# The order of the instructions made by a timeline simulation, in a one-block hybrid kernel

## The chip, the core and the metric

The kernel runs on one core of a Trainium2 chip. The core has five engines, each with an instruction queue of its own that is worked off in order: PE (TensorE, matmuls; its weight loads are listed apart, as PEld), DVE (VectorE), ACT (ScalarE), POOL (GpSimd) and SP (SyncE, which here only issues DMAs). An instruction waits at the head of its queue until the instructions of other engines that it depends on are done, and everything behind it in that queue waits with it. PE writes its results into PSUM, from where DVE and ACT take them to SBUF. The metric is the time of the program on the device in microseconds.

## The reference

One block on 512 tokens of width 1024, with 16 meta tokens put in front: a norm, an input projection, a gated linear recurrence, a retention (linear attention with decay) of 4 heads, a gated mix of the two, and a feed-forward part with a short convolution. All is float32.

```python
xn = rms_norm(h, norm_mix_g[l])
z = xn @ w_in[l]
u_rnn, u_gate, q, k, v, g_ret, ga, gb = jnp.split(z, IN_SPLITS, axis=-1)
xr = causal_dwconv(u_rnn, rnn_conv_w[l], rnn_conv_b[l])
hr = rg_lru(xr, rg_a_w[l], rg_a_b[l], rg_x_w[l], rg_x_b[l], lru_lambda[l])
o_a = hr * jax.nn.gelu(u_gate)
q = rotary(q.reshape(bsz, t, RET_HEADS, RET_DK), pos)
k = rotary(k.reshape(bsz, t, RET_HEADS, RET_DK), pos) * (RET_DK ** -0.5)
o = retention(q, k, v.reshape(bsz, t, RET_HEADS, RET_DV))
o_b = head_rms(o).reshape(bsz, t, RET_HEADS * RET_DV) * jax.nn.silu(g_ret)
mixed = (jax.nn.sigmoid(ga) * (o_a @ w_branch_rnn[l]) + jax.nn.sigmoid(gb) * (o_b @ w_branch_ret[l]))
h = h + mixed @ w_out[l]
xn = rms_norm(h, norm_ffn_g[l])
up = causal_dwconv(xn @ w_up[l], ffn_conv_w[l], ffn_conv_b[l])
gate, val = jnp.split(up, 2, axis=-1)
h = h + (jax.nn.gelu(gate) * val) @ w_down[l]
out = rms_norm(h, norm_final_g)[:, N_META:]
```

## The kernel before

**Numbers.** A float32 operand is split into two float16 parts, a high and a low one (`split`, L91 to L93): ACT writes the high part (L92), DVE the rest (L93). A product is then three passes: high by high, high by low, low by high. Weights come from memory as float32 tiles named `raw`, are split into tiles named `wt`, and stay only as long as they are used; so a stream of weight splits runs on ACT and DVE beside all other work. For some weights sums of blocks are made first (L255 to L257), for a scheme in which 7 block products do the work of 8; `fast_products` (L836), `up_products` (L1314) and the down projection (L1412) use it, the first with tiles `pa`, `pe`, `pb` in PSUM, from which ACT (`kept`, `last`, L849 and L1325) and DVE (`g`, L866, L870, L877) take the sums.

**Stages** (times of the profiled execution, in us): first norm and convolution of the recurrence (0 to 110, L515 to L665), its gates (to 150, L691), rotary products for q and k (145 to 230, `rotary` L720, products in `project` L395, DVE rows L736 to L738), scores and values (230 to 290), values, retention and gated units by head (to 430; values L907, the short product for the meta tokens L899, the sum of squares over a head L944, retention L929), mix units (430 to 650, branch products `pm` L395), output projection (650 to 700, L1180), up projection with its convolution (700 to 955; product L395 or L408, the first tap of the convolution on ACT L1295, the two others on DVE L1297), down projection (955 to 1054, L1417), and a last block of four plain products (L1429) with the final norm and the output (L1513 to L1532).

**Buffers.** PSUM tiles come from pools with few slots: `acc` has 4 slots in the rotary stage (L663), 2 in the gated units beside 4 single banks (L1014), 3 from the output projection on (L1170). A product that takes a slot waits until the last reader of the tile that had it is done. Weight tiles come from a pool of 10 (L60).

**What sets the order.** The kernel is written with a tile framework: the program text names operations in one order, and the framework then orders each engine's queue itself, by priorities and an account of what each instruction takes and when it could start. Two things limit it. From L477 to L713 (`tc.manual_schedule`) the order of PE, DVE and ACT is that of the program text; that part ends near 150 us. And single calls are held with `tc.issue_after` (the loads, L102) or put forward with `tc.high_priority` (L1187, L1251, L1324, L1328). The rows between are free to move. For the up projection two generators give rows in between: `x2_sums` (L1206) makes the sums of normalised activations (`x2t`, L1214 and L1216) and splits them (`x2f`, L93), and `x2_whole` (L1198, row L1204) the sums of high and low part they start from. The last four plain products are written in the order spare, P1, P6, P7 (L1514; spare is the second half of the tile P3).

## Time and profile before

| | |
|---|---|
| median of 3 runs | 1072.78 us (1072.77 to 1072.82) |
| the profiled execution | 1072.88 us, its span 1071.2 us |
| PE busy | 1051.1 us, 8995 matmuls |
| DVE busy | 863.1 us, 1297 instructions |
| ACT busy | 584.1 us, 903 instructions |
| mean granted PE clock | 0.999 of full speed |
| last matmul ends | 1064.6 us |

Busy times are sums over the span from the first to the last instruction. A group of rows is one line, engine and tile; a row of the timeline has start, length, engine, line, the tiles written and read, shapes, a count, and in brackets the idle time before it with what ended it. Rows that follow each other on DVE overlap by some 0.08 us, so the step from one start to the next is a little shorter than the length shown. A wait is counted at the engine that was idle.

### The profile page before, as it was taken

To read this page: it belongs to the slowest core of one execution; us is meant where nothing else is said; L and a number is where in the kernel's file an instruction comes from. 1 tells how busy PE (TensorE), PEld (TensorE's weight loads), DVE (VectorE), ACT (ScalarE), POOL (GpSimd) and SP (SyncE) were. 2 spreads that over 40 slices of the span, in tenths; PEclk is the share of its full clock that TensorE was granted. 3 is DMA by queue.
4 is the path that set the end of the run, shared out by engine and by line. 5 is a ranking of instruction groups with operands and counts; after the bars stand their busy time and mean duration, and the time that the engine had idled before them with its cause. 6 is when DMAs were issued, how large, how long until landed. Compare 5 with 4: busy or idle time off the path is not lost.

```text
span 1071.2 us, 20996 instructions
## 1 busy us (share of the span) xinstructions
PE 1051.1 (98%) x8995; PEld 851.3 (79%) x8995; DVE 863.1 (81%) x1297; ACT 584.1 (55%) x903; POOL 6.9 (1%) x20
## 2 busy tenths in 40 slices
PE   9999999999999999999999999999999999999997
PEld 6888888865684858888888885588888888888884
DVE  6884799998786969877797785599888887988875
ACT  8558954434564747566454453364555465454442
POOL 2000000000000000000000000000000000000000
PEclk9999999999999999999999999999999999999999
DMA  8341243431212222423333355032331423214322
GB/s 254 105 133 41 80 138 119 159 120 40 80 41 69 90 64 65 128 90 119 103 104 119 119 199 176 33 124 74 126 119 62 137 80 119 80 59 131 107 80 79
DMA packets 108990, 111.49 MB, mean 104 GB/s; under 512 B 5611, under 2 KB 100561, under 8 KB 108897
## 3 DMA queue, kind: packets, MB, share of 16 engines
q1 hardware_dynamic: 108448, 109.74, 31.8%
q8 instruction: 70, 1.15, 0.5%
q10 hardware_dynamic: 160, 0.27, 0.1%
q0 software_dynamic: 288, 0.14, 0.1%
q14 instruction: 24, 0.19, 0.1%
HBM read 108.04 MB, written 2.10 MB: 103 GB/s over the span
## 4 chain that ended last, share of the span: by engine, by line
PE 73%; DVE 16%; ACT 9%; issue 2%; ACTq 0%; DVEq 0%
PE ps L395 28%; PE P L1417 9%; PE pa L844 9%; PE pm L395 4%; PE ps L907 4%; PE ps L1180 4%; DVE wt L93 4%; PE pe L844 4%; PE ps L408 2%; PE pb L844 2%; ACT wt L92 2%; PE pa L1319 2%; PE ps L929 1%; DVE rnn L642 1%; DVE raw L255 1%
## 5 line engine op out<-in xcount | busy, mean ns | idle before, releaser
L395 PEld LDWEIGHTS <-wt 128*128 128x128 f16 x3840 | 373.2, 97 | 58.2 <-DVE t L736 1.4
L93 DVE SCALAR_TENSOR_TENSOR wt<-raw,wt 128x1024 f16<-128x1024 f32 (+2 forms) x278 | 303.8, 1105 | 69.1 <-ACT wt L92 68.0
L92 ACT ACTIVATE wt<-raw 128x1024 f16<-128x1024 f32 (+2 forms) x278 | 262.9, 961 | 152.6 <-PE P L1417 25.3
L844 PEld LDWEIGHTS <-wt 128*128 128x128 f16 x2016 | 195.1, 97 | 34.7 <-issue 7.4
L395 PE MATMUL ps<-x2h,wt 128*128 128x258 f16 x1184 | 182.0, 273 | 0.0
L395 PE MATMUL ps<-xh,wt 128*128 128x257 f16 (+2 forms) x1056 | 163.8, 275 | 1.1 <-DVE t L736 1.1
L395 PE MATMUL ps<-x2l,wt 128*128 128x258 f16 x592 | 113.3, 272 | 0.0
L395 PE MATMUL ps<-xl,wt 128*128 128x257 f16 (+2 forms) x528 | 102.2, 275 | 0.0
L1417 PE MATMUL P<-wt,act 128*128 128x256 f16 x792 | 88.3, 273 | 0.0
L1417 PEld LDWEIGHTS <-act 128*128 128x128 f16 x792 | 77.5, 98 | 9.0
L907 PE MATMUL ps<-wt,xh 128*128 128x512 f16 x256 | 76.1, 379 | 2.3 <-DVE v L93 2.3
L844 PE MATMUL pa<-xs,wt 128*128 128x257 f16 x576 | 71.6, 273 | 3.4 <-ACT kept L849 3.1
L1297 DVE SCALAR_TENSOR_TENSOR cv<-ps,vt,cv 128x512 f32<-128x512 f32 x80 | 59.7, 746 | 16.5 <-ACT cv L1295 15.8
L395 PE MATMUL pm<-oa,wt 128*128 128x257 f16 x480 | 55.4, 274 | 0.0
L907 PEld LDWEIGHTS <-xh 128*128 128x128 f16 x256 | 24.8, 98 | 31.4 <-issue 3.4
L907 PE MATMUL ps<-wt,xl 128*128 128x512 f16 x128 | 48.3, 379 | 0.0
L255 DVE TENSOR_TENSOR raw<-raw 128x1024 f32<-128x1024 f32 x39 | 47.6, 1220 | 0.7
L844 PE MATMUL pa<-ob,wt 128*128 128x257 f16 x384 | 45.7, 274 | 0.6 <-ACT last L849 0.5
L1180 PE MATMUL ps<-wt,mx 128*128 128x512 f16 x192 | 44.3, 379 | 0.0
L1295 ACT ACTIVATE cv<-ps,vt,vt 128x512 f32<-128x512 f32 x40 | 30.8, 769 | 23.4 <-PE ps L395 18.5
L1319 PEld LDWEIGHTS <-wt 128*128 128x128 f16 x336 | 32.6, 97 | 8.5 <-issue 4.1
L1180 PEld LDWEIGHTS <-mx 128*128 128x128 f16 x192 | 17.6, 98 | 18.5
(288 smaller groups left out, 1414.6 us busy)
## 6 DMA issues: line engine op xcount, KB each, us to landing
raw<-in_w_in SPq DMA_DIRECT2D x40, 1024.0 KB, 4.9
raw<-in_w_up SPq DMA_DIRECT2D x24, 1024.0 KB, 5.3
raw<-in_w_down SPq DMA_DIRECT2D x48, 256.0 KB, 3.5
raw<-in_w_branch_ret SPq DMA_DIRECT2D x16, 512.0 KB, 4.6
raw<-in_w_branch_rnn SPq DMA_DIRECT2D x8, 640.0 KB, 4.7
raw<-in_w_out SPq DMA_DIRECT2D x4, 1024.0 KB, 5.1
xin<-in_x SPq DMA_DIRECT2D x4, 512.0 KB, 5.8
raw<-in_w_in SPq DMA_DIRECT2D x4, 512.0 KB, 8.3
```

What stands on the lines that cost most here:

```text
L92: nc.scalar.activation(hi, src, AF.Copy, scale=s)
L93: nc.vector.scalar_tensor_tensor(lo, src, s, hi, op0=ALU.mult, op1=ALU.subtract)
L255: nc.vector.tensor_tensor(pair, pair, rv[:, :, right].rearrange("p (h k) c -> p h k c", h=2), op=ALU.add)
L395: nc.tensor.matmul(ps[:, hf, :n], w(aw, k, col, P), src(ax, k, c0, n), start=k == 0 and (aw, ax) == (0, 0), stop=k == nk - 1 and aw == 1)
L408: mm = nc.tensor.matmul(ps[:, hf, :n], w(aw, k, col, P), src(ax, k, c0, n), start=k == 0 and (aw, ax) == (0, 0), stop=k == KD - 1 and aw == 1)
L844: nc.tensor.matmul(ps[:, :257], ws[k // 4](wf, aw, k % 4), src(xf_, ax, k), start=first and k == 0 and (aw, ax) == (0, 0), stop=k == last_ ...
L907: nc.tensor.matmul(pb, xf(ax, k, XF + j0, nb), w(aw, k % 4, 0, 512), start=i == 0, stop=i == 23)
L1180: nc.tensor.matmul(ps[:, n], mx[k][:, a, c0:c0 + P], wo[k // 2](aw, k % 2, n * 512, 512), start=k == 0 and (a, aw) == (0, 0), stop=k == ks ...
L1295: nc.scalar.activation(vv_, src[:, :, 2:258], AF.Identity, scale=vt2[:, 96 + ch:97 + ch], bias=bias)
L1297: nc.vector.scalar_tensor_tensor(vv_, src[:, :, j:j + 256], vt2[:, 48 * j + ch:48 * j + ch + 1], vv_, op0=ALU.mult, op1=ALU.add)
L1319: nc.tensor.matmul(ps[:, :258], w(wf, aw, k), x2_form(xf_, ax, k), start=first and k == 0 and (aw, ax) == (0, 0), stop=k == 3 and aw == 1, ...
L1417: nc.tensor.matmul(pd[:, 256 * tt:256 * tt + 256], t[:, ax, c0 + tt * P:c0 + tt * P + P], w(wf, aw, i), start=q % 6 == 0 and tt == 0 and i ...
```

## The change

One argument is added where the framework is started; the program text of the kernel is the same.

```diff
@@ -1574,7 +1574,7 @@
-    with tile.TileContext(nc) as tc:
+    with tile.TileContext(nc, schedule_with_timeline_sim=True) as tc:
         hybrid_block_kernel(tc, *args)
```

With it the framework keeps a simulated timeline of the engines while it orders the rows that are free to move, in place of its default account. The compiled program has the same instructions with the same shapes, by count and by kind on every engine, and the same 31 loads of activation tables on ACT. What differs is the order in which they stand on PE, DVE and ACT (from DVE's rows near 135 us, ACT's near 145 us and PE's near 230 us on), and two of the last output DMAs on SP. The loads keep their order. Three places follow; numbers behind names tell tiles apart.

The first place is DVE in the rotary stage. `t1_1969` is the product of the second half of q's first head with the cosines, and reads the PSUM tile `ps_1912`; `rnn` tiles belong to the recurrence (L642 its scan, which the profile calls TENSOR_TENSOR_SCAN, L641 its input, L709 its gate), `wt` tiles are weight splits. Before:

```order
L93 SCALAR_TENSOR_TENSOR wt_2037<-raw_1907,wt_2037 128x1024
L642 SCALAR_TENSOR_TENSOR rnn_1039<-rnn_1282,rnn_1521 128x528
L641 TENSOR_TENSOR rnn_1523<-rnn_1523,rnn_1115 128x528
L737 TENSOR_TENSOR t2_1965<-ps_1912,rope1_1851 128x514
L642 SCALAR_TENSOR_TENSOR rnn_1115<-rnn_1357,rnn_1523 128x528
L738 TENSOR_TENSOR t1_1964<-t1_1964,t2_1965 128x514
L736 TENSOR_TENSOR t1_1969<-ps_1912,rope0_1850 128x514
```

and now:

```order
L93 SCALAR_TENSOR_TENSOR wt_2037<-raw_1907,wt_2037 128x1024
L93 SCALAR_TENSOR_TENSOR wt_2089<-raw_1907,wt_2089 128x1024
L709 TENSOR_TENSOR rnn_1653<-rnn_1653,rnn_876 128x514
L642 SCALAR_TENSOR_TENSOR rnn_955<-rnn_1209,rnn_1519 128x528
L641 TENSOR_TENSOR rnn_1521<-rnn_1521,rnn_1039 128x528
L93 SCALAR_TENSOR_TENSOR wt_2173<-raw_2035,wt_2173 128x1024
L93 SCALAR_TENSOR_TENSOR wt_2225<-raw_2035,wt_2225 128x1024
L737 TENSOR_TENSOR t2_1965<-ps_1912,rope1_1851 128x514
L736 TENSOR_TENSOR t1_1969<-ps_1912,rope0_1850 128x514
```

Three weight splits and (counting those further up) three rows of L709 moved ahead of `t1_1969`; two scans, one L641 and one L738 moved behind it.

The second place is PE in the unit of head 2. `ps_4021` and `ps_4084` are two PSUM tiles of the values product, used for two blocks of tokens each; `ps_4145` is the short product for the meta tokens. Before:

```order
L907 MATMUL ps_4084<-wt_3942,xh_95 128x512
L907 LDWEIGHTS xl_96
L907 MATMUL ps_4084<-wt_3942,xl_96 128x512
L899 LDWEIGHTS xlast_2880
L899 MATMUL ps_4145<-wt_3859,xlast_2880 32x512
```

and now:

```order
L907 MATMUL ps_4021<-wt_3942,xh_95 128x512
L907 LDWEIGHTS xl_96
L907 MATMUL ps_4021<-wt_3942,xl_96 128x512
L899 LDWEIGHTS xlast_2880
L899 MATMUL ps_4145<-wt_3859,xlast_2880 32x512
```

The short product follows the second block of `ps_4021` directly now; before, seven matmuls of `ps_4084` stood between. In the same way `ps_4186` (L944) follows `ps_4084` directly, where nine matmuls of a gated unit stood between.

The third place is DVE at the start of the up projection. `cv_8430`, `cv_8475` and `cv_8510` are the convolutions of the first three products, which read `ps_8304`, `ps_8329` and `ps_8371`, the three slots of the pool; each has two rows of L1297. `x2t` and `x2f` are the rows of `x2_sums`. Before:

```order
L93 SCALAR_TENSOR_TENSOR wt_8657<-raw_8515,wt_8657 128x1024
L1297 SCALAR_TENSOR_TENSOR cv_8430<-ps_8304,vt2_94,cv_8430 128x512
L93 SCALAR_TENSOR_TENSOR x2f_8441<-x2t_8400,x2f_8440 128x516
L1297 SCALAR_TENSOR_TENSOR cv_8430<-ps_8304,vt2_94,cv_8430 128x512
L1214 TENSOR_TENSOR x2t_8398<-x2t_8296,x2t_8398 128x516
L1297 SCALAR_TENSOR_TENSOR cv_8475<-ps_8329,vt2_94,cv_8475 128x512
```

and now:

```order
L1214 TENSOR_TENSOR x2t_8402<-x2t_8300,x2t_8402 128x516
L93 SCALAR_TENSOR_TENSOR x2f_8441<-x2t_8400,x2f_8440 128x516
L1216 SCALAR_TENSOR_TENSOR x2t_8296<-x2t_8400,x2t_8296 128x516
L1297 SCALAR_TENSOR_TENSOR cv_8430<-ps_8304,vt2_94,cv_8430 128x512
L93 SCALAR_TENSOR_TENSOR x2f_8441<-x2t_8404,x2f_8440 128x516
L93 SCALAR_TENSOR_TENSOR x2f_8443<-x2t_8398,x2f_8442 128x516
L1216 SCALAR_TENSOR_TENSOR x2t_8300<-x2t_8404,x2t_8300 128x516
L1297 SCALAR_TENSOR_TENSOR cv_8475<-ps_8329,vt2_94,cv_8475 128x512
L93 SCALAR_TENSOR_TENSOR wt_8839<-raw_8655,wt_8839 128x1024
L1216 SCALAR_TENSOR_TENSOR x2t_8298<-x2t_8296,x2t_8298 128x516
L93 SCALAR_TENSOR_TENSOR x2f_8443<-x2t_8402,x2f_8442 128x516
L1297 SCALAR_TENSOR_TENSOR cv_8430<-ps_8304,vt2_94,cv_8430 128x512
```

The rows of `x2_sums` and three weight splits, `wt_8717`, `wt_8779` and `wt_8839`, moved ahead of the second row of `cv_8430`, thirteen rows with the first of `cv_8475`. Beside these, the four last products of PE came as half of P1, P3, the rest of P1, P6, P7, and come as P1, P6, one matmul of P7, P3, the rest of P7; DVE still takes P3 first there.

## The prediction

> **What bounds the kernel now.** First the page: its span, the busy times, the slices.
>
> ```profile
> span 1071.2 us, 20996 instructions
> PE 1051.1 (98%) x8995; PEld 851.3 (79%) x8995; DVE 863.1 (81%) x1297; ACT 584.1 (55%) x903; POOL 6.9 (1%) x20
> DVE  6884799998786969877797785599888887988875
> ```
>
> PE is busy in 1051.1 of 1071.2 us. As every matmul stays, at most those 20.1 us can be won, and a later PE moves the end one for one. DVE has 208 us free in sum, but its slices reach 9 in places. Next, what PE waits for, in all:
>
> ```profile
> PE pa L844 <- ACT kept L849: 3.1, 5, 1.1
> PE pa L1319 <- ACT kept L1325: 2.6, 4, 0.7
> PE ps L907 <- DVE v L93: 2.3, 3, 1.4
> PE ps L475 <- DVE warm L470: 1.5, 1, 1.5
> PE ps L395 <- DVE t L736: 1.1, 1, 1.1
> PE ptr L360 <- DVE xo L353: 0.6, 1, 0.6
> PE pa L844 <- ACT last L849: 0.5, 1, 0.5
> ```
>
> Columns: sum in us, times, longest. Without L475, which stands at the start in the part ordered by hand, these are 10.2 us; that is about what a perfect order could give back in the middle. Last, windows over the stages (length, then busy of PE, PEld, DVE, ACT, POOL, the clock, DMA):
>
> ```profile
> 160.00:180.00 20.00, 18.90 (x169) 16.11 (x168) 20.00 (x30) 9.06 (x13) 0.00 (x0) 1.00 0.32 107
> 283.00:430.00 147.00, 143.24 (x1216) 105.86 (x1214) 119.98 (x182) 89.09 (x153) 0.00 (x0) 1.00 0.24 77
> 430.00:650.00 220.00, 217.34 (x1938) 188.92 (x1938) 173.06 (x233) 117.34 (x178) 0.00 (x0) 1.00 0.39 125
> 700.00:724.00 24.00, 23.35 (x212) 20.36 (x210) 24.00 (x38) 14.51 (x20) 0.00 (x0) 1.00 0.28 89
> 760.00:930.00 170.00, 167.27 (x1496) 145.01 (x1494) 141.55 (x210) 93.26 (x138) 0.00 (x0) 1.00 0.33 106
> ```
>
> In the first and the fourth, DVE is busy without a gap: there a row put ahead of one that PE needs costs PE its full length. In the others DVE is free for 18 to 21% and can take it.
>
> **The change part by part.** No instruction is added or removed; the list and durations stay, so the busy sums cost nothing. What changes is who stands behind whom. I go through the places where PE meets another engine's row.
>
> *Rotary, 160 to 175.* PE's third rotary product may start when `t1_1969` (L736) has read its PSUM tile.
>
> ```profile
> 155.63 1.22 DVE L93 SCALAR_TENSOR_TENSOR wt<-raw,wt 128x1024 f16<-128x1024 f32 x1
> 156.77 1.25 DVE L642 TENSOR_TENSOR_SCAN rnn<-rnn 128x528 f32<-128x528 f32 x1
> 157.94 0.68 DVE L641 TENSOR_TENSOR rnn<-rnn 128x528 f32<-128x528 f32 x1
> 158.54 0.68 DVE L737 TENSOR_TENSOR t<-ps,rope 128x514 f32<-128x514 f32 x1
> ...
> 160.30 0.67 DVE L738 TENSOR_TENSOR t<-t,t 128x514 f32<-128x514 f32 x1
> 160.89 0.68 DVE L736 TENSOR_TENSOR t<-ps,rope 128x514 f32<-128x514 f32 x1
> ...
> 166.86 0.68 DVE L709 TENSOR_TENSOR rnn<-rnn 128x514 f32<-128x514 f32 x1
> 161.63 0.40 PE L395 MATMUL ps<-xh,wt 128*128 128x257 f16 x2 [1.10 <-DVE t L736]
> ```
>
> From start to start a weight split takes 1.14, a scan 1.17, L641, L709 and L738 0.60. Ahead of `t1_1969` now stand three more splits (3.4) and three more L709 (1.8), and two scans (2.3), one L641 and one L738 (1.2) fewer: +1.7. The same count up to `t1_2097`, which frees the fifth product's tile, is +3.4; before it had 0.7 to spare. So **+2.8**, bounds 0 and 3.4.
>
> *Values and gated units, 283 to 430.* 147 − 143.24 = 3.8 us of waits can go. But the short product `ps_4145` (L899) now stands directly behind the values product whose tile it shares, where 7 matmuls of another stood between, and `ps_4186` (L944) directly behind the next, where 9 stood. Each waits for a split of v on ACT and then on DVE:
>
> ```profile
> L93 DVE SCALAR_TENSOR_TENSOR v<-ps,v 128x512 f16<-128x512 f32 x20 | 13.4, 684 | 13.8 <-ACT v L92 13.8
> ```
>
> 0.68, and about as long before it on ACT: 1.3. Three such places (heads 2 and 3) wait the 1.3, and a fourth, where ten matmuls stand between, 0.4: 4.3. A gate product near 420, whose drain now stands behind a weight split on DVE, adds 1.3, short waits for kept 0.5, and half a weight split ahead of the other drains 0.7; less the 3.8 saved: **+3.0**, bounds −3.8 and 7.5 (nothing saved but the same waits and some more).
>
> *Mix units, 430 to 650.* 220 − 217.34 = 2.7 can go; products of different units are now interleaved and some drains come 1 to 4 us later on engines that are free for a fifth of the time. **+0.5**, bounds −2.7 and 4; I take a value near zero as DVE's 47 us of idle time covers most.
>
> *Up-projection, 700 to 724: the largest term.* The fourth up product (`ps_8523`) needs the tile of the first, free when the second tap of `cv_8430` (L1297) is done.
>
> ```profile
> 711.09 0.74 DVE L1297 SCALAR_TENSOR_TENSOR cv<-ps,vt,cv 128x512 f32<-128x512 f32 x1
> 711.75 0.68 DVE L93 SCALAR_TENSOR_TENSOR x2f<-x2t,x2f 128x516 f16<-128x516 f32 x1
> 712.35 0.74 DVE L1297 SCALAR_TENSOR_TENSOR cv<-ps,vt,cv 128x512 f32<-128x512 f32 x1
> 713.01 0.68 DVE L1214 TENSOR_TENSOR x2t<-x2t 128x516 f32<-128x516 f32 x1
> 713.61 0.74 DVE L1297 SCALAR_TENSOR_TENSOR cv<-ps,vt,cv 128x512 f32<-128x512 f32 x1
> 714.33 0.39 PE L395 MATMUL ps<-x2h,wt 128*128 128x258 f16 x2
> ```
>
> The tap of 712.35 ended at 713.0 and PE came at 714.33: 1.3 us to spare. Now thirteen rows that stood behind that tap stand ahead: three L1214, three L1216 and three x2f splits at 0.60 to 0.61, another tap 0.66, three weight splits at 1.14, in all 9.5. One split (`wt_8779`) also waits some 1.6 for its ACT half, which waits for PE. So 713.0 + 9.5 + 1.6 = 724.1 against 714.33: **+9.8**, bounds 0 (DVE reaches the tap early) and 12. About 2.0 of it lie earlier, at 706.5, where PE waits for an x2l split that stood at 704.5 and now stands behind four more rows; the rest is one wait of 7 to 8 us. Nothing hides it: DVE is at 24.00 of 24.
>
> *The clock after that wait.* No wait of PE in this trace is over 1.5 us, but the end shows what a pause does. The last matmul ends at 1064.6, and the clock column falls from the fourth microsecond on:
>
> ```profile
> 1067.00:1068.00 1.00, 0.00 (x0) 0.00 (x0) 0.28 (x1) 0.51 (x1) 0.00 (x0) 1.00 0.13 47
> 1068.00:1069.00 1.00, 0.00 (x0) 0.00 (x0) 0.00 (x0) 0.00 (x0) 0.00 (x0) 0.65 0.88 328
> 1069.00:1070.00 1.00, 0.00 (x0) 0.00 (x0) 0.00 (x0) 0.00 (x0) 0.00 (x0) 0.50 0.52 197
> 1.50 4.88 PE L475 MATMUL ps<-warm 128*128 128x512 f16 x11 [1.50 <-DVE warm L470]
> 1061.87 1.46 PE L1429 MATMUL P<-wt,a 128*128 128x512 f16 x6
> 1063.16 1.46 PE L1429 MATMUL P<-wt,act 128*128 128x512 f16 x6
> ```
>
> The first eleven matmuls of 512 columns take 4.88 us, 0.44 each; six late ones take 1.29, 0.215 each. So a start from rest costs 11 × 0.22 = **+2.4**; bounds 0 (it stays up, or the wait is under 3.7) and 2.4. [...]
>
> *Four fast units, 760 to 930.* 170 − 167.27 = 2.7 us of waits for kept (the 2.6 above) can go; instead a product waits about 1.3 for a conv tap behind a weight split, once in a unit, and some of it is covered: **+1**, bounds −2.7 and 5.
>
> *Tail.* The plain products came as P1, P3, P6, P7 in part; now P3, which DVE still takes first, comes after P1 and P6.
>
> ```profile
> 1058.18 0.69 DVE L1521 SCALAR_TENSOR_TENSOR hu<-P,h 128x512 f32<-128x512 f32 x1 [2.84 <-PE P L1429]
> 1058.91 0.69 DVE L1524 TENSOR_TENSOR h<-hu,gfin 128x512 f32<-128x512 f32 x1
> 1059.52 0.68 DVE L1521 SCALAR_TENSOR_TENSOR hu<-P,h 128x512 f32<-128x512 f32 x1
> ...
> 1066.79 0.48 DVE L1529 TENSOR_SCALAR h<-h,rs 128x512 f32<-128x512 f32 x1
> ```
>
> P3 ends 19 matmuls of 0.215 later, so DVE starts at 1062.3; three sums, three weighings, a scaling and a reciprocal (4.3, at the pitches above) put the last sum at 1066.6, and 2.5 more us of DVE rows put the last scaling at 1069.1 instead of 1066.79: **+2.3**, bounds 0 and 3.
>
> Sum: 2.8 + 3.0 + 0.5 + 9.8 + 2.4 + 1 + 2.3 = 21.8. The profiled run took 1072.88 us (span 1071.2 and 1.7 around it), 0.1 over the median of 1072.78, so **1094.7**.
>
> **The rivals.**
> *Faster:* DVE reaches the tap of `cv_8430` and `t1_1969` before PE, because the rows moved ahead found their operands earlier and fill its 208 idle us; then PE's waits of the middle go and none comes. 1072.9 − 10.2 = 1062.7. It decides by whether that tap ends ahead of PE's arrival, 714.33; the 24.00 of 24 speaks against it, PE's few long waits for it.
> *Waits saved pay for the small terms:* the three stages of the middle give all their idle time, −3.8 − 2.7 − 2.7 = −9.2, and rotary, up-projection, clock and tail stay at 17.3: 1081.0. For it: DVE and ACT have idle time there. Against: the rows behind `ps_4145` leave PE nothing to do.
> *More new waits:* gated 7.5, mix 4, fast units 5, the rest as summed: 17.3 + 16.5 = 33.8, so 1106.7. For it: in-order queues pass a late row on.
> *Nothing:* only rows that PE never waits for change, 1072.9. Against: the order of PE itself.
>
> **How the numbers follow.** Forecast 0.62, saved waits 0.15, more waits 0.12, faster 0.08, nothing 0.03. The forecast's own range is 1086 to 1104, from the bounds of the gated, up-projection and clock terms not all being met at once. To hold 8 in 10 the range takes in the saved waits and half of the more: 1078 to 1107. A difference under 0.2% (2.1 us) could not be told from none. Faster 0.08, within 0.2% 0.03, slower 0.89.
>
> **What would show it.** In the changed profile PE should wait once for 7 us or more at L395 near 730 (for DVE cv L1297), with the clock at 0.50 in part of the next 5 us; some 3 us at L395 near 165 to 178 for DVE t L736; L899 and L944 about 1.3 each for DVE v L93; and the last L1529 some 4.5 us after the last matmul. The forecast fails if the tile of `ps_8523` isn't the one `cv_8430` frees, or if DVE had room in 700 to 724 that the records don't show.

## The result and the profile after

The changed kernel took 1104.81 us, the median of four runs from 1103.03 to 1106.64; the kernel before took 1072.78 on the same chip (1072.70 to 1072.82). The ratio is 1.0297, with a 95% interval from 1.0283 to 1.0312. The profiled execution took 1105.44 us, with a span of 1103.7 against 1071.2: 32.5 us more, where 21.8 were forecast. The time lies in the stated range, and the sign was right; it lies just above the forecast's own range of 1086 to 1104, and the size of several terms was wrong.

The page of the changed kernel, its span and busy times:

```profile
span 1103.7 us, 21012 instructions
PE 1055.3 (96%) x8995; PEld 854.0 (77%) x8995; DVE 864.8 (78%) x1297; ACT 581.0 (53%) x903; POOL 6.9 (1%) x20
```

The instructions are the same 8995, 1297 and 903. PE's idle time is now 1103.7 − 1055.3 = 48.4 us, against 20.1 before, so 28.3 of the 32.5 us are idle time of PE, 3.9 of them behind its last matmul. The other 4.2 are PE's own busy time, though it does the same products: some ran at a lower clock. What PE waits for, in the view of the waits (sum, times, longest):

```profile
PE ps L395 <- DVE cv L1297: 11.8, 5, 5.3
PE ps L395 <- DVE t L736: 3.8, 2, 2.8
PE ps L944 <- DVE v L93: 3.5, 2, 1.7
PE pa L844 <- ACT kept L849: 3.1, 4, 1.5
PE pa L844 <- ACT last L849: 3.0, 1, 3.0
PE pe L844 <- DVE g L866: 2.4, 2, 1.2
PE ps L408 <- DVE x2l L93: 1.7, 1, 1.7
PE ps L899 <- DVE v L93: 1.7, 2, 1.4
PE ps L929 <- DVE v L93: 1.5, 1, 1.5
PE ps L475 <- DVE warm L470: 1.5, 1, 1.5
PE ps L929 <- ACT rt L946: 1.4, 1, 1.4
```

Of the old waits, those for kept at L1325 (2.6) and for v at L907 (2.3) are gone; L475 at the start and the sum for kept at L844 (3.1) are as before; the rest of this list is new or longer. To place the loss in the program, one follows the same product of PE through both traces and notes how much later it starts. This table is worked out from the start times of nine such products:

| product, start before and after | late by | stage that ends there |
|---|---|---|
| `ps_2122`, 161.63, 163.19 | 1.6 | |
| first scores, 226.50, 229.25 | 2.8 | rotary 2.8 |
| first retention, 285.66, 289.98 | 4.3 | (scores, 1.6 of the gated 9.5) |
| mix unit, 472.51, 484.74 | 12.2 | gated 9.5 |
| output projection, 649.32, 662.34 | 13.0 | mix 0.8 |
| `ps_8523`, 714.33, 735.88 | 21.6 | |
| `ps_8601`, 719.68, 743.98 | 24.3 | up 11.3 |
| down projection, 953.20, 981.85 | 28.7 | fast units 4.3 |
| last matmul, 1064.24, 1092.87 | 28.6 | down 0.0 |
| end of the span, 1071.2, 1103.7 | 32.5 | tail 3.9 |

**Up projection.** The timeline of PE and that of DVE just ahead of it (start, length):

```profile
735.88 0.61 PE L395 MATMUL ps<-x2h,wt 128*128 128x258 f16 x2 [5.31 <-DVE cv L1297]
```

```profile
726.63 1.22 DVE L93 SCALAR_TENSOR_TENSOR wt<-raw,wt 128x1024 f16<-128x1024 f32 x1 [0.64 <-ACT wt L92]
...
729.59 0.74 DVE L1297 SCALAR_TENSOR_TENSOR cv<-ps,vt,cv 128x512 f32<-128x512 f32 x1
730.25 1.29 DVE L93 SCALAR_TENSOR_TENSOR x2f<-x2t,x2f 128x516 f16<-128x516 f32 x2
731.46 0.69 DVE L1216 SCALAR_TENSOR_TENSOR x2t<-x2t 128x516 f32<-128x516 f32 x1
732.07 0.74 DVE L1297 SCALAR_TENSOR_TENSOR cv<-ps,vt,cv 128x512 f32<-128x512 f32 x1
732.73 1.22 DVE L93 SCALAR_TENSOR_TENSOR wt<-raw,wt 128x1024 f16<-128x1024 f32 x1
733.86 0.69 DVE L1216 SCALAR_TENSOR_TENSOR x2t<-x2t 128x516 f32<-128x516 f32 x1
734.47 0.69 DVE L93 SCALAR_TENSOR_TENSOR x2f<-x2t,x2f 128x516 f16<-128x516 f32 x1
735.07 1.41 DVE L1297 SCALAR_TENSOR_TENSOR cv<-ps,vt,cv 128x512 f32<-128x512 f32 x2
```

Between the first tap of `cv_8430` (729.59) and its second (735.07) DVE now works through splits, sums and another tap without a gap, and PE starts right when the tap's 0.74 us are over. It is the wait that the forecast named, 5.3 instead of 7 to 8 us.

**The clock.** The times at which the granted clock changes in this trace lie apart by multiples of one stretch: 656.26, 659.67, 721.11, 724.52, 734.76 and 741.59 are 1, 18, 1, 3 and 2 times 3.41 us from each other. The windows below are such stretches, some ahead of a change and some behind it (length; busy time and count of PE, PEld, DVE, ACT, POOL; the clock; DMA):

```profile
161.32:164.74 3.42, 1.55 (x14) 1.37 (x15) 3.42 (x6) 2.00 (x2) 0.00 (x0) 1.00 0.52 170
...
652.84:656.26 3.42, 0.89 (x9) 0.78 (x8) 2.16 (x3) 2.27 (x3) 0.00 (x0) 1.00 0.30 83
656.26:659.67 3.41, 3.41 (x18) 2.39 (x16) 1.85 (x4) 0.84 (x2) 0.00 (x0) 0.50 0.75 271
...
717.70:721.11 3.41, 1.69 (x13) 1.15 (x12) 3.41 (x7) 1.18 (x2) 0.00 (x0) 1.00 0.96 303
721.11:724.52 3.41, 3.31 (x16) 2.35 (x16) 3.41 (x7) 0.00 (x0) 0.00 (x0) 0.50 0.03 8
...
731.35:734.76 3.41, 0.00 (x0) 0.00 (x0) 3.41 (x6) 1.62 (x4) 0.00 (x0) 1.00 0.00 0
734.76:741.59 6.83, 5.71 (x27) 4.04 (x28) 6.66 (x11) 3.97 (x6) 0.00 (x0) 0.50 0.49 154
741.59:745.00 3.41, 3.41 (x33) 2.94 (x32) 2.18 (x4) 1.43 (x4) 0.00 (x0) 1.00 0.02 5
...
946.39:949.80 3.41, 1.61 (x15) 1.44 (x16) 3.41 (x6) 1.69 (x3) 0.00 (x0) 1.00 0.02 5
```

A full stretch holds some 33 matmuls at clock 1.00 and some 18 at 0.50. Taken as half of the busy time at 0.50 (an estimate from these counts), each place loses: 1.7 after the wait of 3.0 us at 655, 1.7 after the wait of 1.7 at 721, 2.9 after the wait of 5.3. That is 6.2 in three places, where the forecast had 2.4 in one. In this trace the falls go with how much of one stretch PE stood idle: 2.5 us (656.26) and 3.4 (734.76) were followed by a fall, while the waits of 2.8 at 163 and of 2.7 at 948, each cut in two by the end of a stretch, left 1.9 and 1.8 in the longer part, and the clock stayed up. The fall at 721.11, after 1.7 of idle time, is the odd one; 1.2 us of transposes (L360) stand in the same stretch.

The busy sum shows only 4.2 more. Two other things make it smaller. At the start full speed came earlier than in the trace of before, though no row there has changed: the first eleven matmuls start 0.43 us apart there, and here 0.22 apart from the eighth on (4.39), so they took 1.0 us less (4.88 before):

```profile
1.50 3.92 PE L475 MATMUL ps<-warm 128*128 128x512 f16 x11 [1.50 <-DVE warm L470]
```

And a matmul's record lasts 0.27 us where the next one starts 0.11 later; ahead of a short pause the last record counts in full, so that 0.16 of the pause is booked as busy. In the mix stage the trace of before has eleven such pauses and that of the changed kernel one: 1.6 us. This is also why the mix stage is only 0.8 late: its idle time went from 2.1 to 3.0, and the fall of 1.7 stands against these 1.6. The 0.6 that is left of 6.2 − 1.0 − 1.6 against 4.2 is spread over the other stages.

**Gated units.** Two windows over the stage, in the changed kernel:

```profile
286.00:360.00 74.00, 67.22 (x569) 48.72 (x567) 51.51 (x75) 40.64 (x70) 0.00 (x0) 1.00 0.24 81
360.00:442.00 82.00, 75.08 (x631) 56.00 (x632) 64.61 (x94) 46.34 (x78) 0.00 (x0) 1.00 0.19 61
```

PE is idle for 6.8 + 6.9 = 13.7 us, against 3.8 before (283 to 430), at full clock. From the list above, L944 (3.5), kept (3.1), g (2.4), L899 (1.7) and the two of L929 (2.9) make 13.6. No single one is over 1.8 us.

**Tail.** Three rows of the last norm, and one window after them:

```profile
1090.91 0.69 DVE L1521 SCALAR_TENSOR_TENSOR hu<-P,h 128x512 f32<-128x512 f32 x1 [6.72 <-PE P L1429]
...
1098.25 0.48 DVE L1529 TENSOR_SCALAR h<-h,rs 128x512 f32<-128x512 f32 x1
...
1099.00 0.39 ACTq L1532 DMA_DIRECT2D out<-h  x1
```

```profile
1100.00:1101.00 1.00, 0.00 (x0) 0.00 (x0) 0.00 (x0) 0.00 (x0) 0.00 (x0) 0.50 1.01 383
```

DVE waits 6.7 us for P3, then all four sums follow each other. The last scaling is 31.46 us later than before (1066.79), 2.8 more than PE. From it to the end of the span it takes 5.45 us, before 4.4: five output DMAs are issued between 1097.4 and 1099.0 and still move 383 GB/s two microseconds later.

### The profile page after: what moved, and what is told of

Its sections match the earlier page's. It is cut to its first block, busy times and chain, and to the rows that moved or that the text cites. A ratio compares the mean times of both kernels' runs of the same rounds, so it can differ in the third digit from the quotient of the medians.

```text
span 1103.7 us, 21012 instructions
## 1 busy us (share of the span) xinstructions
PE 1055.3 (96%) x8995; PEld 854.0 (77%) x8995; DVE 864.8 (78%) x1297; ACT 581.0 (53%) x903; POOL 6.9 (1%) x20
## 4 chain that ended last, share of the span: by engine, by line
PE 73%; DVE 15%; ACT 8%; DMA 2%; issue 2%; ACTq 0%; DVEq 0%
PE ps L395 25%; PE pa L844 9%; PE P L1417 9%; PE ps L907 7%; PE pm L395 5%; DVE wt L93 5%; PE pe L844 4%; PE ps L1180 3%; ACT wt L92 2%; PE pb L844 2%; PE pa L1319 2%; DVE cv L1297 2%; PE ps L408 2%; PE ps L781 1%; DVE rnn L642 1%
## 5 line engine op out<-in xcount | busy, mean ns | idle before, releaser
L844 PEld LDWEIGHTS <-wt 128*128 128x128 f16 x2016 | 196.2, 98 | 38.5 <-issue 9.8
L395 PE MATMUL ps<-x2h,wt 128*128 128x258 f16 x1184 | 185.2, 275 | 12.7 <-DVE cv L1297 11.8
L907 PE MATMUL ps<-wt,xh 128*128 128x512 f16 x256 | 76.5, 379 | 0.0
L844 PE MATMUL pa<-xs,wt 128*128 128x257 f16 x576 | 71.8, 273 | 3.1 <-ACT kept L849 3.1
L1297 DVE SCALAR_TENSOR_TENSOR cv<-ps,vt,cv 128x512 f32<-128x512 f32 x80 | 59.0, 748 | 15.6 <-ACT cv L1295 14.9
L844 PE MATMUL pa<-ob,wt 128*128 128x257 f16 x384 | 47.4, 280 | 3.0 <-ACT last L849 3.0
L907 PE MATMUL ps<-wt,xl 128*128 128x512 f16 x128 | 48.5, 379 | 0.0
L907 PEld LDWEIGHTS <-xh 128*128 128x128 f16 x256 | 24.6, 98 | 28.6 <-issue 1.7
L929 PE MATMUL ps<-sc,v 128*128 128x257 f16 (+4 forms) x384 | 32.1, 236 | 3.1 <-DVE v L93 1.5
```

What stands on the lines that cost most here:

```text
L395: nc.tensor.matmul(ps[:, hf, :n], w(aw, k, col, P), src(ax, k, c0, n), start=k == 0 and (aw, ax) == (0, 0), stop=k == nk - 1 and aw == 1)
L844: nc.tensor.matmul(ps[:, :257], ws[k // 4](wf, aw, k % 4), src(xf_, ax, k), start=first and k == 0 and (aw, ax) == (0, 0), stop=k == last_ ...
L907: nc.tensor.matmul(pb, xf(ax, k, XF + j0, nb), w(aw, k % 4, 0, 512), start=i == 0, stop=i == 23)
L929: nc.tensor.matmul(ps[:, hf, s0 - lo_i:257], vt[b][:, va, d * P:(d + 1) * P], st[SCP[b][0]][:, sa, o:o + hi_i - s0], start=i == 0, stop=i ...
L1297: nc.vector.scalar_tensor_tensor(vv_, src[:, :, j:j + 256], vt2[:, 48 * j + ch:48 * j + ch + 1], vv_, op0=ALU.mult, op1=ALU.add)
```

## The experiments

The main theory: only the order of the rows costs, and the loss is a sum of stages as in the table, each mended by giving that stage the order of before. Rivals: the switch does something else as well; one engine's queue alone carries the loss; a loss mended in one place comes back behind it.

Eight kernels hold rows of the changed kernel in the order of before. The program is first traced without the argument, for the order; then with it, and edges which fix only the order within one engine's queue chain the rows of a part:

```diff
+    with tile.TileContext(nc) as tc:
+        hybrid_block_kernel(tc, *args)
+        traced = {i.name: k for k, i in enumerate(tc.nc.cur_bb.bb.instructions)}
+    rows = [...]                  # the order of before
     with tile.TileContext(nc, schedule_with_timeline_sim=True) as tc:
         hybrid_block_kernel(tc, *args)
+        hold(tc, rows, parts, engines)
...
+def hold(tc, rows, parts, engines):
...
+            if ins.engine in last:
+                tc.add_manual_dep(ins, last[ins.engine].name, mybir.DependencyInfo(
+                    mybir.DependencyClass.NoSync, mybir.DependencyReason.DATA), reason="held")
+            last[ins.engine] = ins
```

The marks for the parts move the line numbers in these kernels by up to 6 (L844 is L846 there, L1297 is L1303).

**All rows held** (every part from rotary on; PE, DVE and ACT):

> The changed kernel, in which PE, DVE and ACT are held to the order of before from the rotary stage to the end. Theory A (only the order costs): the time of before, 1072.8 us within 0.2%. Rival (the switch changes something besides the order, buffers or waits): clearly above 1075.

Measured 1073.14 us (median of 10, 1072.91 to 1075.07), ratio 1.0006 [0.9997, 1.0016]. With the switch on and the old order the time is the old one: the cost is the order, nothing else.

**Only PE's rows held, and only DVE's and ACT's:**

> The changed kernel with PE alone held to the order of before; DVE and ACT are ordered by the simulation around it. Counted from the two traces the change costs 2.8 us in the rotary stage, 9.6 in values and gated units, 0.8 in the mix, 11.3 at the start of the up projection, 4.4 in the fast units and 3.9 in the tail. Theory A (PE's order costs in gated units, fast units and tail, DVE's rows in rotary and up projection): 2.8 of rotary stay, the up projection keeps about 2 as three sums and one split still stand ahead of the tap (2.9 less 1.3 of cover): about 1078 (1075 to 1083). Rival (DVE's and ACT's order costs everywhere, whatever PE does): 1095 or more.

> The changed kernel with DVE and ACT held to the order of before, and PE ordered by the simulation around them. Theory A: rotary 2.8 and up projection 11.3 go, and part of the rest as PE's rows follow the drains: 1080 to 1090. Rival (it is DVE's and ACT's order everywhere): 1073 to 1076. Rival (PE's order alone): 1095 or more.

In both the main theory was missed. The times are those of the rivals, but each rival puts the whole loss on the other engines' order, and both can't be so; neither holds. With PE's old order alone: 1097.38 us, ratio 1.0231 [1.0215, 1.0246]; with DVE's and ACT's alone: 1097.16, ratio 1.0229 [1.0214, 1.0245]. Each half alone leaves some 24.6 us of the loss, though not the same waits. The waits with PE's order of before and the others' new:

```profile
PE pa L846 <- ACT kept L851: 7.5, 6, 2.4
PE pa L1325 <- ACT kept L1331: 6.5, 4, 2.0
PE ps L909 <- DVE v L93: 4.9, 4, 1.8
...
PE ps L395 <- DVE t L737: 2.8, 1, 2.8
```

and with DVE's and ACT's order of before and PE's new:

```profile
PE pa L846 <- ACT kept L851: 8.3, 9, 2.4
PE ps L783 <- DVE v L93: 4.1, 2, 2.3
PE ps L946 <- DVE v L93: 2.8, 2, 1.4
PE ps L901 <- DVE v L93: 2.8, 2, 1.4
...
PE ps L395 <- DVE t L737: 1.4, 1, 1.4
```

The waits for cv, 11.8 us, are all but gone in both (the second has 1.1 of them). The rotary wait goes only with DVE's order (1.4 instead of 2.8), the waits at the short product (L901, L899 elsewhere) only with PE's. But the waits for kept in the gated and mix units, 3.1 before, more than double in both: ACT drains the products in one order, PE makes them in another. 24.6 + 24.6 is more than 32, so the loss isn't shared out between the engines; a queue is right or wrong only together with the queues that it meets.

**One stage held, on all three engines.** Four stages and the tail, one each:

> The changed kernel, in which only the rows traced for the rotary stage are held to the order of before. Theory A (DVE's three weight splits and three L709 ahead of t L736 cost 2.8 at once and nothing later): 1102.0 (1100.5 to 1103.5), PE's waits for DVE t L736 back to one of about 1.1. Rival (the splits done early spare a later wait, so it is partly given back): 1104 to 1106.

> The changed kernel, in which only the rows traced for the retention, values and gated units (PE, DVE and ACT) are held to the order of before. Theory A (the 9.6 us lost between 283 and 472 come from the order of these rows): 1104.8 - 9.6 = 1095.2 (1093 to 1097), without PE's waits for DVE v L93 at L944 and L899 over 0.5. Rival (weight splits of other stages that stand between them, and are not held, keep most of it): 1100 or more.

> The changed kernel, in which only the rows traced from the start of the up projection up to its third unit are held to the order of before (PE, DVE and ACT). Theory A (the sums and splits ahead of the tap cost 11.3 us here, with the clock): 1104.8 - 11.3 = 1093.5 (1092 to 1095), and PE's wait for DVE cv L1297 at 736 is gone. Rival (the time lost here is lost again behind it, as the later stages were waiting anyway): 1098 or more.

> The changed kernel, in which only the rows traced for the units 3 to 9 of the up projection are held to the order of before. Theory A (the waits of 0.6 to 2.8 for cv in each fast unit less the four waits for kept that were saved, 4.4 in all): 1100.4 (1099 to 1102). Rival (these waits are a late effect of the wait at 736 and stay): no change, 1104 to 1106.

> The changed kernel, in which only the rows of the last four plain products and what follows them are held to the order of before (PE, DVE and ACT; SP's output DMAs stay as ordered by the simulation). Theory A (P3 third instead of second makes DVE's rows queue behind it, 2.8 us, and the output DMAs start together and end 1.0 us later for it): 1104.8 - 3.9 = 1100.9 (1099.5 to 1102.5). Rival (the end is set by the output DMAs whatever the order of the products): 1104 or more.

| held | measured, us (runs) | gives back | late by the table | the stage loses in its own trace |
|---|---|---|---|---|
| rotary | 1102.89 (1102.00 to 1103.34) | 1.9 | 2.8 | 0.1 |
| gated | 1096.87 (1093.75 to 1098.72) | 7.9 | 9.5 (7.9 from the first retention on) | 0.1 from the first retention on |
| up | 1095.92 (1094.66 to 1098.85) | 8.9 | 11.3 | 0.7 |
| fast units | 1100.66 (1100.33 to 1102.88) | 4.2 | 4.3 | 1.3 |
| tail | 1099.98 (1098.64 to 1102.14) | 4.8 | 3.9 | 0.0 |

The last column is the table of start times made again from the trace of each held kernel.

The gains are against 1104.81; the runs of before on these chips gave 1072.59 to 1072.63. Together the five give back 27.7 of the 32.0 us. Four of the five lie in the ranges of their theories; the up stage, at 1095.92 against 1092 to 1095, does not. In its own trace each held stage is rid of most of its loss or all of it; what comes back at the end differs from that by up to 1.7 us, and the runs of one kernel differ by 1.3 to 5.0. For the gated units there is a reason: 1.5 of their 9.5 us are the wait for v that ends at 289.98, ahead of the rows that were held, and their trace still has it (1.5 at 290.05). With the up stage held, its wait of 5.3 us is gone and `ps_8523` is 12.6 us late instead of 21.6; a wait of 1.3 us for xo stands ahead of it, and in its profiled execution the clock fell in other places than in the changed kernel. One of them is the rotary wait, which this kernel shares with the changed one. Two stretches with the up stage held:

```profile
159.83:163.25 3.42, 0.64 (x6) 0.31 (x4) 3.42 (x5) 0.78 (x1) 0.00 (x0) 1.00 0.64 209
163.25:166.66 3.41, 3.40 (x16) 2.39 (x17) 3.41 (x5) 1.23 (x2) 0.00 (x0) 0.50 0.89 300
```

Here the whole wait of 2.8 us falls into one stretch; in the changed kernel the end of a stretch at 161.32 cuts it. The same wait for the same tile at the same time costs 1.7 us more in one execution than in the other, by the clock alone (half of the 3.40 us that PE was busy at 0.50). That also fits the spread of the changed kernel (3.6 us among four runs, 0.1 for before, where no wait in the middle is over 1.5 us): in order of their times, 1103.03, 1104.18, 1105.44 and 1106.64, the four runs had a mean clock of 0.994, 0.991, 0.991 and 0.989.

**A wait made by hand in the kernel of before**, to price a wait and the clock fall by themselves: extra scalings by 1.0 on DVE between the taps of the first convolution, twelve, then six.

```diff
         for j in (1, 0):
             nc.vector.scalar_tensor_tensor(vv_, src[:, :, j:j + 256], ...)
+            if ch == 0 and j == 1:
+                for _ in range(12):
+                    nc.vector.tensor_scalar_mul(cv[:, :SEQ], cv[:, :SEQ], 1.0)
```

> The kernel before, with twelve extra rows on DVE (a scaling by 1.0 of the first convolution, 128x512, in place) between its two taps of L1297, so that the tile for the fourth up product comes free later. A row of that shape took 0.48 us at L1529, so about 5.8 to 6 us more work against 1.3 of cover: PE waits 4.5 to 4.7. Theory A (a wait costs its length and then the price of a lower clock, 2.6 as after the wait at 736): 1072.7 + 7.2 = 1079.9 (1079 to 1081), the clock at 0.50 for about 5 us. Rival (the wait costs its length alone): 1077.3.

> The same with six extra rows: 2.9 to 3 us against 1.3 of cover, so a wait of about 1.7. Theory A in the form the traces give it (the clock falls after some waits of 1.9 to 3 us and not after others): 1074.4 if it stays up and 1076 if it falls, so runs that differ by over 1 us. Rival (only waits above 3.7 us lower it): 1074.4 in every run.

Both were missed: twelve rows gave 1076.78 (1075.55 to 1076.98), ratio 1.0035 [1.0021, 1.0048]; six gave more, 1078.36 (1078.23 to 1078.99), ratio 1.0053 [1.0039, 1.0067]. The framework spread the extra rows over the queue: the last of the twelve starts at 723.03, and PE's product, at 715.49, did not wait for them, so it must have taken the slot of another product. The wait at that place was only 0.93 us with twelve rows:

```profile
715.49 0.40 PE L395 MATMUL ps<-x2h,wt 128*128 128x258 f16 x2 [0.93 <-DVE cv L1297]
...
773.51 0.71 PE L1322 MATMUL pa<-x2f,wt 128*128 128x258 f16 x5 [2.20 <-ACT kept L1328]
```

and a second wait came 58 us further on, in rows that the edit doesn't touch. With six rows the second wait was this one, with the window behind it:

```profile
951.62 0.40 PE L395 MATMUL ps<-x2h,wt 128*128 128x258 f16 x2 [2.50 <-DVE cv L1297]
```

```profile
952.00:954.00 2.00, 2.00 (x12) 1.42 (x10) 1.05 (x3) 0.72 (x2) 0.00 (x0) 0.50 0.06 19
```

With twelve rows the profiled execution is the fastest of the four, and its clock stayed up; the other three, at a mean clock of 0.996 to 0.997 instead of 0.999, took 1.0 to 1.4 us more. A price of a wait made by hand was not had; what these runs show is that a wait of 2.5 us can take the clock along, and that an edit to one engine's rows reorders others.

**An order better than both?** In the kernel of before PE's largest waits are those for kept (3.1 and 2.6 us). In `up_products`, and then in `fast_products` too, the product T2 was written one place later, so that B21 would stand between the drain of one product and the next:

```diff
-        product(pa, "T2", "F6")
-        keep(kept[:, 1], pa)
-        yield
         pb = bank("pb")
         product(pb, "B21", "A12", True)
         add(g0[:, 0], pb, kept[:, 0])
         yield
+        product(pa, "T2", "F6")
+        keep(kept[:, 1], pa)
+        yield
```

> The kernel before (default order), with the second and third product of a fast up unit exchanged in the program text, so that two products and not one stand between the two uses of the tile pa. Theory A (PE waits for what stands directly ahead in its own queue; the four waits for kept, 2.6 in all, go as nothing else waits there): 1070.1 (1069.5 to 1071). Rival (ACT or DVE is late anyway and the wait moves to the next product): 1072 to 1073.5.

> The same exchange in the fast units of the gated and mix stages too, where PE waited 3.1 for kept. Theory A: 2.6 + 3.1 less a little: 1067.5 (1066.5 to 1069.5). Rival (the default order fits the old text, and moved rows bring new waits): 1071 or more.

Neither was a gain: 1073.27 us, ratio 1.0006 [0.9997, 1.0015], and 1076.47, ratio 1.0034 [1.0021, 1.0047]. The first tested nothing: its trace has the rows of PE, DVE and ACT in the same order as before, since the default order had already put B21 ahead of T2 there, and the waits for kept in the fast units stayed (2.6 in four). The second made the gated ones longer, from 3.1 to the 5.0 of this row of its waits,

```profile
PE pa L844 <- ACT kept L849: 5.0, 8, 0.8
```

while those for v at L907 fell from 2.3 to 1.1. That is 0.7 us of waits for a kernel 3.7 slower. Its PE counts 1053.8 us of busy time, 2.7 more, at a clock of 1.00; where a product waits for its drain, 24 matmuls count as 2.82 us busy, where it doesn't they take 2.66, so part of each short pause is booked as busy. Its trace has eleven such pauses more, 1.8 of the 2.7; where the rest lies is open. No version here beats the kernel of before.

## Why the prediction was right, and where its sum was off

- **What bounds the kernel** held: PE's lateness sets the end, and no busy sum of DVE or ACT mattered. Holding the order gave everything back, so the order is the cause; whether the right rows were named is a matter of each stage.
- **Rotary**, forecast 2.8: 2.8 in the trace; 1.9 came back when the stage was held, and its trace has lost the lateness up to 0.1. The count of DVE rows ahead of `t1_1969` and `t1_2097` was right (waits 2.8 and 1.0).
- **Values and gated units**, forecast 3.0 with an upper bound of 7.5: 9.5, and 7.9 came back in the run. This is the term that was mis-sized most. The prediction subtracted all 3.8 us of old waits and counted 6.8 of new ones. The old ones were not saved as a sum: 2.3 at L907 went, but those for kept stayed at 3.1. Of the new ones, L899 and L944 were counted at 4.3 and came to 5.2, the gate product at 1.3 and came twice (2.4); the two at L929 (1.5 and 1.4, for v and rt) weren't counted, since only the two moved short products were looked at, and not what a late short product holds up behind it. The first of the two lies ahead of the rows that were held for this stage, and stayed.
- **Mix units**, forecast 0.5: 0.8. The size is right, but its make-up is not: it holds a wait of 3.0 us for the last drain and a clock fall of 1.7, against 2.1 us of old idle time and 1.6 of short pauses gone. That it came out near 0.5 is luck.
- **Up-projection wait and clock**, forecast 9.8 + 2.4 = 12.2: 11.3, of which 8.9 came back. The wait at L408 for x2l came as said (1.7, forecast 2.0), the wait for `cv_8430` came at the named row, but 5.3 and not 7 to 8. One part of that is `wt_8779`: DVE waited 0.64 for its ACT half, not 1.6. Another is that the clock fell at 721 already, so PE itself came later to the place and had less to wait: with the gated units held, where the clock was at 0.59 from 714 to 717, the wait was 5.3 as well, and with the rotary stage, the fast units or the tail held it was 6.2. That the sum came near is in part luck: the wait was shorter than said, and the clock took 1.7 + 2.9 here instead of 2.4.
- **The clock** was the step with the wrong condition. The prediction let only waits over 3.7 us count and priced one place. In the trace it fell after 1.7, 3.0 and 5.3 us, and stayed up after 2.8 (at 163) and after another of 2.7 in the last fast unit. The price was no fixed one either: it was read from the start, where the same eleven matmuls took 4.88 us in the trace of before and 3.92 in that of the changed kernel. Two things were in no term of the forecast: the changes of the clock lie apart by multiples of 3.41 us, and the fall at 656.26 came after 2.5 us of idle time in the stretch ahead of it.
- **Fast units**, forecast 1: 4.3, and 4.2 came back. The waits for kept went as said (2.6 before). But PE waits for cv twice in each of three units: 0.4 (for ACT's row, L1311) and 1.2, the same again, and 2.7 and 1.4 in the last, together 7.4 with rounding. The prediction had one wait of 1.3 per unit, and let most of it be covered.
- **Tail**, forecast 2.3: 3.9; 4.8 came back in the run, within its spread. The late P3 cost 2.8. The output DMAs that now stand together at the end cost another 1.0; the prediction ended at the last scaling.
- **The rivals.** That saved waits pay for the small terms fell most clearly: 4.9 were saved (L907 and L1325), while the gated and fast units got 13.6 − 3.1 + 7.4 = 17.9 of new ones. More new waits, at 1106.7, was nearer in size than the forecast; its reason, in-order queues that pass a late row on, is what the gated and fast units show. So the time lies in the stated range because that range took in half of this rival.

The sum: gated +6.5, fast units +3.3, tail +1.6, mix +0.3, up and clock −0.9 against the forecast make 10.8, the gap of 10.7 from 21.8 to 32.5 but for rounding. What stays open: why the clock fell after the wait of 1.7 us at 721, and 4.3 us of the 32.0 that no single held stage gave back. Of these the mix units (0.8) and the wait ahead of the first retention (1.5) were in no held stage; the other 2.0 are within the spread of the runs.

## What to carry to other kernels

When only an order changes, follow one engine's rows through the stages, and ask at each meeting of two queues whether both moved in step; half of an order brings back little (1097 for either half, 1073 for both, 1105 for none). Count new waits at every row that a moved row feeds, not at that row alone, and take old waits as saved only where their own cause is gone. In a kernel like this one, with PE 98% busy, add a charge for the clock to each wait of the size that a fall followed here (1.7, 2.5, 3.0 and 5.3 us), 1.7 us for a short one, as a chance and not as a sum: the same wait of 2.8 us paid it in one execution and not in another.

## What the runs showed of the hardware

In the changed kernel the granted clock fell to 0.50 for 3.41 us after the waits of 3.0 us at 655 and of 1.7 at 721, and for 6.83 us after the one of 5.3 at 736; the falls cost 1.7, 1.7 and 2.9 us by the estimate above. Behind the last product it fell too, 3.3 us after that product's end at 1093.25, and in the kernel of before 3.7 us after 1064.62. The traces of before and after, cut into stretches of 3.41 us from the start of the first clock record on (6.75 and 4.31), have four stretches at full clock in which PE was idle for 2.5 us or more (2.5, 3.3, 3.4 and 3.4); each was followed by one at 0.50. Of the 623 others, with 1.9 us of idle time or less, one was: the one from 717.70, with 1.7 us idle and 1.2 of transposes besides. This row of the changed kernel ends a wait of 2.7 us that no slower matmul followed; 1.8 of it lie in the stretch from 946.39, shown above:

```profile
948.19 0.38 PE L395 MATMUL ps<-x2h,wt 128*128 128x258 f16 x2 [2.68 <-DVE cv L1297]
```

The output DMAs, when five are issued within 1.6 us, ran at 369 to 383 GB/s from 1098 to 1102; the span ended 1.7 us later. With the tail held to the order of before, where two are issued behind the last scaling, the end came 4.4 us behind it and not 5.45.
